# Attention layers: the high and low parts of q made by VectorE in place of GpSimd

## Chip, cores and metric

The kernel runs on one NeuronCore of a Trainium2 chip. The metric is the device time of one launch in microseconds (us); a run's time is that of its slowest core, here the only one. The engines are TensorE (PE in the rows; PEld is its loading of stationary operands), VectorE (DVE), ScalarE (ACT), GpSimd (POOL) and SyncE (SP), which issues most transfers. Each engine executes its own instructions in program order, and semaphores order the engines among each other.

## What is computed

The reference is one inference step of a decoder trunk of four layers (attention, a gated recurrence, a short gated convolution, attention), each followed by a SwiGLU feed-forward block, on 512 prompt tokens and 8 x 8 decode tokens, with model width 1024. All is float32. The change lies in the attention layers (0 and 3), cut here to what matters:

```python
qkv = h @ w_qkv + b_qkv
q = rope(q, pos); k = rope(k, pos)          # 16 query heads, 2 key/value heads, width 64
s = einsum(q, k) * 64 ** -0.5               # sliding window of 128 keys
p = softmax(concat([where(mask, s, -1e30), sink]))[..., :-1]
out = einsum(p, v) @ w_o + b_o
```

## The kernel before

The tokens are handled in two groups g of 288 columns (256 prompt tokens and 32 decode tokens). Activations lie transposed, features on the 128 partitions, so that a weight tile of 128 output features meets 288 columns. To get float32 accuracy out of single-pass matmuls every operand is split into a high part (the value rounded to fp32r, by a cast) and a low part (what the rounding left, by a subtraction); one product then takes three matmuls (lines 443 to 445: high by high, low by high, high by low). ScalarE casts each weight tile (`wh`, line 361), and the remainder `wl` is subtracted by VectorE (line 368) or, for the nine tiles from v and q of each attention layer and some others, by GpSimd in two halves of 128x512 (line 365).

In an attention layer a projection unit per head pair c and group g fills one PSUM bank (24 matmuls). Its evacuation `q_evac` (line 819) scales the bank (line 507), applies the rotary embedding in `rope` (VectorE at 752, 762 and 763, ScalarE at 757), which leaves the pair's rotated q in a scratch tile t, 128 partitions by 256 prompt columns, and then makes four pieces of 64 partitions by 256 columns. The first head's high part and its remainder go to the two halves of `mh`, the second head's remainder and high part to the two halves of `ml`. ScalarE casts one high part (line 832). GpSimd does the rest: a cast (827) and a subtraction (829) for the first head, in a side task of its own, and a subtraction (834) for the second.

A task per (g, c) then runs the attention itself: eight score matmuls on those pieces (lines 877 and 879), the masked minimum on VectorE (845), the exponential on ScalarE (851), after a GpSimd copy of the sink column into the tile P (883), reciprocal and normalisation on VectorE (855, 859), transposes of P on TensorE (894), a ScalarE copy to PT (896) and the product with v (910). Decode tokens take similar steps (930 to 966). Two P tiles and two PT tiles limit the tasks in flight. The output projection (`out_units`, evacuated at 656) follows and overlaps the last tasks.

The order of all instructions is set before the run by a list scheduler in the file (class `Sched`): each step of each task is yielded with an engine letter (P, A, D, G, S) and a guessed cost in us, and the scheduler picks for each engine the ready step of best priority. A step's guessed cost and engine therefore decide the order on every engine. Pools of eight PSUM banks, ten scratch tiles and six weight slots hold tasks back.

Of the kernel before, what the change touches and what calls it, by code (L numbers as in the profile page):

```python
# [8 lines left out]
F32 = mybir.dt.float32  # L9
# [5 lines left out]
D = 1024  # L15
# [5 lines left out]
HD = 64  # L21
# [3 lines left out]
NP = 256  # L25
# [220 lines left out]
def cA(n, sb=0, ap=0):  # L246
    return n / 1200 + 0.05 + 0.04 * sb + 0.09 * ap


def cD(n, ap=0):  # L250
    return n / 960 + 0.07 + 0.06 * ap


class Builder(Sched):
# [433 lines left out]
    def attention(self, layer, l):  # L688
        nc = self.nc
# [52 lines left out]
        def rope(ps, g, c, tmp, outs, key):  # L742
            b = bq(c)
            raw, rot = yield ("acq", self.scr, 2)
            yield from self.scaled(g, idx, raw, ps)
            yield ("free", self.pp, [ps])
            yield ("wait", [("const", l, "cos")])
            cs, sn = st["cs"][:, g, :], st["sn"][:, g, :]

            def part(out, src, b, t):  # L750
                yield ("D", cD(N, 1))
                nc.vector.scalar_tensor_tensor(out=out, in0=src, scalar=b, in1=t, op0=ALU.add, op1=ALU.mult)
            yield ("spawn", part(tmp, raw, b, cs), None, [("cos",) + key])
            yield ("A", 4 * cA(N, 1))
            for s in range(4):
                d = s ^ 1
                nc.scalar.copy(rot[32 * d:32 * d + 32, :], raw[32 * s:32 * s + 32, :])  # L757
            yield from part(rot, rot, self.cst(f"br{l}", c), sn)
            yield ("wait", [("cos",) + key])
            yield ("D", 0.44)  # L760
            v2 = lambda t: t.rearrange("p (a n) -> p a n", a=2)
            nc.vector.tensor_add(outs[0], tmp[:, :NP], rot[:, :NP])
            nc.vector.tensor_add(outs[1], v2(tmp[:, NP:]), v2(rot[:, NP:]))
            yield ("free", self.scr, [raw, rot])
            yield ("set", key)
# [52 lines left out]
        def q_evac(g, c, ps):  # L818


            [t] = yield ("acq", self.scr, 1)
            yield from rope(ps, g, c, t, (t[:, :NP], st["qs"][g][:, :, c, :]), ("qr", l, g, c))
            mh, ml = (m[:, c, :NP] for m in self.mid[g])

            def first():
                yield ("G", 0.97)
                nc.gpsimd.tensor_copy(mh[:HD], t[:HD, :NP])
                yield ("G", 0.7)
                nc.gpsimd.tensor_sub(mh[HD:], t[:HD, :NP], mh[:HD].bitcast(F32))
            yield ("spawn", first(), None, [("q1", l, g, c)])  # L830
            yield ("A", cA(NP, 1))
            nc.scalar.copy(ml[HD:], t[HD:, :NP])
            yield ("G", 0.7)
            nc.gpsimd.tensor_sub(ml[:HD], t[HD:, :NP], ml[HD:].bitcast(F32))
            yield ("wait", [("q1", l, g, c)])
            yield ("free", self.scr, [t])
            yield ("set", ("q", l, g, c))

# [140 lines left out]
        for c in range(KC):  # L979
            i = self.take()  # L980
            for g in range(2):
                def fn(prio, i=i, g=g, c=c):
                    pt = prio + AOFF[g]
                    self.spawn(task(g, c, pt), pt, 0.0, [("mp", l, g, c)])
                    if c == KC - 1:
                        for p in range(2):
                            ps = prio + SOFF[g] + p
                            self.spawn(stask(g, p, ps), ps, 0.0, [("ms", l, g, p)])
                    return self.unit(i, g, self.h, self.hkeys(g, idx), lambda ps: q_evac(g, c, ps), step=STEP)
                self.add(g, fn)  # L990
# [690 lines left out]
```

## Time and profile before

| | |
|---|---|
| time, median of 3 runs | 2393.68 us (2393.63 to 2394.46) |
| time of the profiled execution | 2392.32 us |
| span of the profiled execution | 2390.5 us |
| mean granted TensorE clock | 0.996 of full speed |
| busy, share of the span | PE 98%, DVE 70%, ACT 51%, POOL 28% |

The span runs from the first to the last instruction; the time also holds what lies around it, 1.8 us here. Layer 0's attention lies at the start of the span, up to about 200 us, layer 3's at about 1780 to 1975 us. A row of a wait names the engine and line that ended an engine's idle time. Busy time of PE counts pipelined matmuls that overlap, so a busy PE is not PE at its peak.

### The profile page before, as it was taken

The page shows a single profiled execution, that of the slowest core. Times are in us where ns is not written, and L with a number is a line of the kernel's source. Part 1 is how long each engine was busy: PE and PEld are TensorE (multiplying, and loading weights), DVE is VectorE, ACT ScalarE, POOL GpSimd, SP SyncE. Part 2 cuts the span into 40 slices and gives each one's busy share as a digit, 9 for nine tenths or more (in the row PEclk, how much of TensorE's full clock was granted, in tenths as well). Part 3 has the DMA queues.
Part 4 walks back from the last instruction along what each step waited for, and adds up shares of the span by engine and source line. Part 5 has one row for each costly group of instructions (what it writes and reads, how often), then busy time and mean ns, then how long its engine had stood idle before and what let it go on. Part 6 is the DMA issues. An engine that isn't in the chain of part 4 may idle for free.

```text
span 2390.5 us, 44197 instructions
## 1 busy us (share of the span) xinstructions
PE 2337.0 (98%) x17596; PEld 2300.3 (96%) x17596; DVE 1682.2 (70%) x3253; ACT 1226.8 (51%) x2546; POOL 659.1 (28%) x728
## 2 busy tenths in 40 slices
PE   8999999999999999999999999999999999999998
PEld 7889999999989999999999999999999899999998
DVE  8877848486896784848665578484867868757574
ACT  7864535355587552535422255353548845535353
POOL 5410414150451042424000004241415301333230
PEclk9999999999999999999999999999999999999999
DMA  5112232223222122322322212322242111413231
GB/s 186 46 51 65 71 106 87 86 100 103 63 80 92 53 97 83 103 81 90 109 89 80 82 62 79 99 93 94 87 132 86 46 54 36 137 58 115 71 107 49
DMA packets 64063, 203.69 MB, mean 85 GB/s; under 512 B 11040, under 2 KB 13904, under 8 KB 63840
## 3 DMA queue, kind: packets, MB, share of 16 engines
q1 hardware_dynamic: 62800, 199.52, 25.8%
q8 instruction: 138, 2.26, 0.4%
q0 software_dynamic: 336, 0.61, 0.1%
q10 hardware_dynamic: 720, 0.73, 0.1%
q14 instruction: 69, 0.57, 0.1%
HBM read 197.87 MB, written 4.94 MB: 85 GB/s over the span
## 4 chain that ended last, share of the span: by engine, by line
PE 80%; DVE 12%; ACT 6%; issue 1%; POOL 0%; DMA 0%; DVEq 0%; ACTq 0%; POOLq 0%
PE bank L443 14%; PE bank L444 14%; PE bank L445 14%; PE bank L1373 12%; PE bank L1375 11%; PE bank L1374 11%; DVE wl L418 1%; DVE s L1328 1%; ACT s L757 1%; PE bank L894 1%; DVE cv L1047 1%; ACT P L851 1%; PE bank L910 1%; ACT wh L361 1%; DVE hl L474 1%
## 5 line engine op out<-in xcount | busy, mean ns | idle before, releaser
L443 PE MATMUL bank<-mh,wh 128*128 128x288 f32 x1984 | 589.6, 297 | 4.6 <-ACT rg L1128 2.5
L444 PE MATMUL bank<-ml,wh 128*128 128x288 f32 x1984 | 585.6, 295 | 1.4 <-DVE ml L474 1.4
L445 PE MATMUL bank<-mh,wl 128*128 128x288 f32 x1984 | 583.6, 294 | 0.0
L443 PE MATMUL bank<-hh,wh 128*128 128x288 f32 x1344 | 407.1, 303 | 0.7 <-ACT hh L472 0.4
L444 PE MATMUL bank<-hl,wh 128*128 128x288 f32 x1344 | 399.2, 297 | 7.2 <-DVE hl L474 7.2
L445 PE MATMUL bank<-hh,wl 128*128 128x288 f32 x1344 | 398.4, 296 | 3.4 <-POOL wl L365 2.3
L443 PEld LDWEIGHTS bank<-mh,wh 128*128 128x128 f32 x1984 | 371.8, 187 | 7.0 <-ACT rg L1128 3.0
L361 ACT CAST wh<-raw 128x1024 fp32r<-128x1024 f32 (+2 forms) x217 | 219.2, 1012 | 310.0 <-PE bank L444 250.2
L444 PEld LDWEIGHTS bank<-ml,wh 128*128 128x128 f32 x1984 | 372.4, 188 | 2.3 <-DVE ml L474 1.9
L445 PEld LDWEIGHTS bank<-mh,wl 128*128 128x128 f32 x1984 | 373.5, 188 | 0.0
L418 DVE TENSOR_TENSOR wl<-raw,wh 128x512 fp32r<-128x512 f32 x380 | 347.8, 941 | 13.0 <-ACT wh L416 12.1
L659 DVE TENSOR_TENSOR x<-bank,x 128x288 f32<-128x288 f32 x224 | 102.0, 456 | 272.6 <-PE bank L445 272.6
L416 ACT CAST wh<-raw 128x512 fp32r<-128x512 f32 x380 | 228.5, 616 | 109.8 <-PE bank L444 107.4
L1375 PE MATMUL bank<-hh,wl 128*128 128x288 f32 x912 | 268.7, 295 | 4.8 <-DVE wl L418 4.8
L1373 PE MATMUL bank<-hh,wh 128*128 128x288 f32 x912 | 269.9, 296 | 0.0
L1374 PE MATMUL bank<-hl,wh 128*128 128x288 f32 x912 | 269.0, 295 | 0.0
L368 DVE TENSOR_TENSOR wl<-raw,wh 128x1024 fp32r<-128x1024 f32 (+2 forms) x187 | 222.9, 1192 | 58.8 <-ACT wh L361 56.9
L444 PEld LDWEIGHTS bank<-hl,wh 128*128 128x128 f32 x1344 | 254.7, 189 | 8.5 <-DVE hl L474 7.8
L445 PEld LDWEIGHTS bank<-hh,wl 128*128 128x128 f32 x1344 | 255.3, 190 | 4.8 <-POOL wl L365 3.2
L443 PEld LDWEIGHTS bank<-hh,wh 128*128 128x128 f32 x1344 | 254.4, 189 | 4.6 <-issue 2.2
L1381 ACT COPY s<-bank 128x288 f32<-128x288 f32 x228 | 91.2, 400 | 186.9 <-PE bank L1375 185.8
L1375 PEld LDWEIGHTS bank<-hh,wl 128*128 128x128 f32 x912 | 171.8, 188 | 6.0 <-DVE wl L418 6.0
(371 smaller groups left out, 5035.5 us busy)
## 6 DMA issues: line engine op xcount, KB each, us to landing
raw<-in_w SPq DMA_DIRECT2D x303, 512.0 KB
raw<-in_w SPq DMA_DIRECT2D x64, 448.0 KB
out_y<-x SPq DMA_DIRECT2D x12, 144.0 KB
x<-in_x SPq DMA_DIRECT2D x4, 288.0 KB
x<-in_x SPq DMA_DIRECT2D x2, 576.0 KB
ck<-in_ckt SPq DMA_DIRECT2D x4, 256.0 KB
cv<-in_cv SPq DMA_DIRECT2D x4, 256.0 KB
ca<-in_ca SPq DMA_DIRECT2D x2, 480.0 KB
```

The lines of the kernel that those rows point to most:

```text
L361: self.nc.scalar.copy(fh[:, z], r[:, z])
L368: self.nc.vector.tensor_sub(fl[:, z], r[:, z], fh[:, z].bitcast(F32))
L416: self.nc.scalar.copy(fh, src)
L418: self.nc.vector.tensor_sub(fl, src, fh.bitcast(F32))
L443: mm(out, lhsT=wh(k), rhs=xh(k), start=(k == 0), stop=False)
L444: mm(out, lhsT=wh(k), rhs=xl(k), start=False, stop=False)
L445: mm(out, lhsT=wl(k), rhs=xh(k), start=False, stop=(k == n - 1))
L659: nc.vector.tensor_add(x[:, m, :], ps[:, :N], x[:, m, :])
L1373: mm(ps[:, :N], lhsT=wh[:, k, :], rhs=xh[:, k, :], start=first and k == 0, stop=False, skip_group_check=not first)
L1374: mm(ps[:, :N], lhsT=wh[:, k, :], rhs=xl[:, k, :], start=False, stop=False, skip_group_check=not first)
L1375: mm(ps[:, :N], lhsT=wl[:, k, :], rhs=xh[:, k, :], start=False, stop=k == hk - 1, skip_group_check=not first)
L1381: nc.scalar.copy(c[n], ps[:, :N])
```

## The change

The three GpSimd instructions of a head pair become VectorE instructions with the same operands, and the side task `first` is dissolved: its two steps now stand in line ahead of ScalarE's cast. The scheduler is told 0.22 for the cast and `cD(NP)`, which is 0.337, for a subtraction, where it was told 0.97 and 0.7 of GpSimd. It is done 32 times in a run: 8 head pairs, 2 groups, 2 layers.

```diff
             mh, ml = (m[:, c, :NP] for m in self.mid[g])
 
-            def first():
-                yield ("G", 0.97)
-                nc.gpsimd.tensor_copy(mh[:HD], t[:HD, :NP])
-                yield ("G", 0.7)
-                nc.gpsimd.tensor_sub(mh[HD:], t[:HD, :NP], mh[:HD].bitcast(F32))
-            yield ("spawn", first(), None, [("q1", l, g, c)])
+            yield ("D", 0.22)
+            nc.vector.tensor_copy(mh[:HD], t[:HD, :NP])
+            yield ("D", cD(NP))
+            nc.vector.tensor_sub(mh[HD:], t[:HD, :NP], mh[:HD].bitcast(F32))
             yield ("A", cA(NP, 1))
             nc.scalar.copy(ml[HD:], t[HD:, :NP])
-            yield ("G", 0.7)
-            nc.gpsimd.tensor_sub(ml[:HD], t[HD:, :NP], ml[HD:].bitcast(F32))
-            yield ("wait", [("q1", l, g, c)])
+            yield ("D", cD(NP))
+            nc.vector.tensor_sub(ml[:HD], t[HD:, :NP], ml[HD:].bitcast(F32))
             yield ("free", self.scr, [t])
             yield ("set", ("q", l, g, c))
```

The scheduler's order moves on every engine within the two attention stretches, and outside them PE's order is the same. Lines after 834 carry numbers smaller by 3 in the changed kernel. Three places follow.

VectorE in layer 0, from the end of the first rope evacuation (s_87 is the rotated q of the first head pair, mh_102 and ml_103 are the pieces of group 0). Before:

```order
L762 TENSOR_TENSOR s_87<-s_87,s_89 128x256
L763 TENSOR_TENSOR qs_0_133<-s_87,s_89 128x2x16
L507 TENSOR_TENSOR s_92<-bank_65,rt_108 128x288
L752 SCALAR_TENSOR_TENSOR s_90<-s_92,cpack,cos_118 128x288
L507 TENSOR_TENSOR s_85<-bank_62,rt_107 128x288
```

and in the changed kernel:

```order
L762 TENSOR_TENSOR s_87<-s_87,s_89 128x256
L763 TENSOR_TENSOR qs_0_133<-s_87,s_89 128x2x16
L826 CAST mh_102<-s_87 64x256
L828 TENSOR_TENSOR mh_102<-s_87,mh_102 64x256
L507 TENSOR_TENSOR s_92<-bank_65,rt_108 128x288
L752 SCALAR_TENSOR_TENSOR s_90<-s_92,cpack,cos_118 128x288
L832 TENSOR_TENSOR ml_103<-s_87,ml_103 64x256
L507 TENSOR_TENSOR s_85<-bank_62,rt_107 128x288
```

Three VectorE instructions now stand among the evacuations of the next banks.

GpSimd at the same place (wl are weight remainders, P_0_135 and P_0_137 the two P tiles). Before:

```order
L365 TENSOR_TENSOR wl_80<-raw_72,wh_79 128x512 x2
L827 CAST mh_102<-s_87 64x256
L829 TENSOR_TENSOR mh_102<-s_87,mh_102 64x256
L834 TENSOR_TENSOR ml_103<-s_87,ml_103 64x256
L365 TENSOR_TENSOR wl_82<-raw_69,wh_81 128x512 x2
L883 COPY P_0_135<-cpack 128x4
```

and in the changed kernel:

```order
L365 TENSOR_TENSOR wl_80<-raw_72,wh_79 128x512 x2
L365 TENSOR_TENSOR wl_82<-raw_69,wh_81 128x512 x2
L880 COPY P_0_135<-cpack 128x4
L365 TENSOR_TENSOR wl_84<-raw_70,wh_83 128x512 x2
L880 COPY P_0_137<-cpack 128x4
```

What is left on GpSimd there is weight remainders and sink columns.

TensorE late in layer 0's attention, where the last prompt tasks meet the output projection (its rows have mh and wh; bank_62 and the like are PSUM banks). Before:

```order
L443 MATMUL bank_61<-mh_102,wh_73 128x288
L444 MATMUL bank_61<-ml_103,wh_73 128x288
L445 MATMUL bank_61<-mh_102,wl_74 128x288
L910 MATMUL bank_62<-PT_0_140,vtok_130 64x128 x8
L894 MATMUL bank_64<-ca_117,P_0_135 128x128 x4
L894 MATMUL bank_66<-ca_117,P_0_135 128x128 x4
L877 MATMUL bank_67<-kh_0_122,mh_104 128x256
```

and in the changed kernel:

```order
L445 MATMUL bank_68<-mh_102,wl_74 128x288
L891 MATMUL bank_67<-ca_117,P_0_137 128x128 x4
L891 MATMUL bank_64<-ca_117,P_0_137 128x128 x4
L891 MATMUL bank_65<-ca_117,P_0_135 128x128 x4
L891 MATMUL bank_62<-ca_117,P_0_135 128x128 x4
L907 MATMUL bank_63<-PT_0_140,vtok_130 64x128 x8
L907 MATMUL bank_61<-PT_0_139,vtok_130 64x128 x8
L443 MATMUL bank_66<-mh_102,wh_75 128x288
```

The transposes of two tasks now stand in one block, with both products with v right behind them; before, projection or score matmuls stood between a task's last transpose and its product.

## Rows read from the trace of the kernel before

**Rows 1.** The page's head: span, and busy time by engine.

```profile
span 2390.5 us, 44197 instructions
...
PE 2337.0 (98%) x17596; PEld 2300.3 (96%) x17596; DVE 1682.2 (70%) x3253; ACT 1226.8 (51%) x2546; POOL 659.1 (28%) x728
```

**Rows 2.** Busy us by stretch: PE, PEld, DVE, ACT, POOL, clock, DMA share, GB/s.

```profile
30.00:160.00 130.00, 121.69 (x1016) 111.54 (x1015) 115.86 (x374) 110.90 (x306) 56.35 (x81) 0.99 0.22 67
1810.00:1940.00 130.00, 125.40 (x1059) 115.11 (x1058) 109.33 (x373) 106.86 (x300) 47.87 (x75) 1.00 0.18 59
...
80.00:90.00 10.00, 9.05 (x70) 7.98 (x67) 9.65 (x35) 8.88 (x28) 6.82 (x10) 1.00 0.08 19
...
1890.00:1900.00 10.00, 9.47 (x91) 7.81 (x88) 9.77 (x31) 8.87 (x25) 3.37 (x6) 1.00 0.40 134
```

**Rows 3.** PE's waits from 30 to 160 us: us in total, times, longest.

```profile
PE bank L894 <- DVE P L859: 4.1, 6, 1.4
...
PE bank L877 <- POOL mh L829: 1.0, 1, 1.0
PE bank L944 <- DVE P L859: 0.9, 2, 0.5
```

**Rows 4.** PE's waits from 1810 to 1940 us.

```profile
PE bank L894 <- DVE P L859: 1.4, 3, 0.5
...
PE bank L944 <- DVE P L859: 0.4, 1, 0.4
```

**Rows 5.** GpSimd's groups over the span: busy us, mean ns; idle before.

```profile
L834 POOL TENSOR_TENSOR ml<-s,ml 64x256 fp32r<-64x256 f32 x32 | 26.0, 811 | 6.4 <-ACT ml L832 4.3
L829 POOL TENSOR_TENSOR mh<-s,mh 64x256 fp32r<-64x256 f32 x32 | 25.8, 807 | 2.5
...
L827 POOL CAST mh<-s 64x256 fp32r<-64x256 f32 x32 | 16.1, 503 | 111.5 <-DVE s L762 111.4
```

**Rows 6.** VectorE in order of time: start, duration, undisturbed instructions.

```profile
40.25 0.41 DVE L774 TENSOR_TENSOR kl<-s,kh 64x256 fp32r<-64x256 f32 x1
40.59 0.44 DVE L507 TENSOR_TENSOR s<-bank,rt 128x288 f32<-128x288 f32 x1
...
141.28 0.35 DVE L859 TENSOR_SCALAR P<-P,st 128x256 f32<-128x256 f32 x1
141.55 0.42 DVE L474 TENSOR_TENSOR ml<-bank,mh 128x256 fp32r<-128x256 f32 x1
```

**Rows 7.** VectorE and GpSimd in order of time, where both run.

```profile
34.32 1.09 DVE L752 SCALAR_TENSOR_TENSOR s<-s,cpack,cos 128x288 f32<-128x288 f32 x1
...
35.81 0.52 DVE L752 SCALAR_TENSOR_TENSOR s<-s,cpack,cos 128x288 f32<-128x288 f32 x1
...
34.36 0.74 POOL L829 TENSOR_TENSOR mh<-s,mh 64x256 fp32r<-64x256 f32 x1
```

**Rows 8.** PE in order of time: its waits, in brackets their length and end.

```profile
59.87 0.86 PE L894 MATMUL bank<-ca,P 128*128 128x128 f32 x5 [0.57 <-DVE P L859]
...
71.09 0.30 PE L894 MATMUL bank<-ca,P 128*128 128x128 f32 x1 [1.50 <-ACT P L851]
72.39 0.41 PE L894 MATMUL bank<-ca,P 128*128 128x128 f32 x2 [0.99 <-DVE P L859]
...
1884.07 0.41 PE L894 MATMUL bank<-ca,P 128*128 128x128 f32 x2 [0.43 <-DVE P L859]
...
1942.57 1.09 PE L910 MATMUL bank<-PT,vtok 128*64 128x128 f32 x14 [0.57 <-ACT PT L896]
```

**Rows 9.** GpSimd and VectorE ahead of the wait at 71 us.

```profile
69.60 2.49 POOL L365 TENSOR_TENSOR wl<-raw,wh 128x512 fp32r<-128x512 f32 x2 [0.39 <-POOL mh L829]
...
69.71 2.53 DVE L859 TENSOR_SCALAR P<-P,st 128x128 f32<-128x128 f32 x2
...
46.37 0.55 DVE L859 TENSOR_SCALAR P<-P,st 128x128 f32<-128x128 f32 x2
```

**Rows 10.** The stretch behind that wait, one us: clock 0.50 of full speed.

```profile
73.00:74.00 1.00, 1.00 (x6) 1.00 (x5) 0.93 (x6) 0.81 (x3) 0.00 (x0) 0.50 0.91 176
```

## The prediction

> **What bounds the kernel now.** I read the page's head first: PE is busy 2337.0 us of a span of 2390.5 us, so all of PE's idle time together is 53.5 us [rows 1]. The change touches two stretches only, so the next view is busy time by stretch. From 30 to 160 us (layer 0) PE is idle 130 - 121.69 = 8.3 us, from 1810 to 1940 us (layer 3) 130 - 125.40 = 4.6 us [rows 2]. These 12.9 us are nearly all that a change here can win, 0.5% of the time, since the matmuls themselves stay the same. VectorE is the next engine: busy 115.86 and 109.33 us of 130, against 56.35 and 47.87 of GpSimd [rows 2]. The waits of PE tell what VectorE's delay costs: 4.1 + 0.9 us in layer 0 and 1.4 + 0.4 us in layer 3, 6.8 us together, end when VectorE has normalised P; a single one, of 1.0 us, ends with GpSimd's low part of q [rows 3, 4].
>
> **What leaves GpSimd.** 32 casts and 64 subtractions, 16.1 + 25.8 + 26.0 = 67.9 us of its busy time [rows 5]. None of it is time by itself, since GpSimd waits more than it works here. Three things come with it.
>
> The wait on GpSimd's low part goes: 1.0 us [rows 3]. In its place the first scores wait for VectorE's three instructions; these stand two to four places behind the rope sum in the order shown, while on GpSimd the three take 0.50 + 0.81 + 0.81 = 2.1 us by their means [rows 5], one after the other. I take the whole 1.0 us as won.
>
> VectorE's own instructions get faster. An L752 that takes 0.52 us alone took 1.09 us while GpSimd's L829 ran [rows 7]. Going through VectorE's rows of both layers I find 21 such, from that one at 34.32 us to one at 1890.41 us, that ran long beside one of the three instructions and beside no weight remainder; what they took over their undisturbed length sums to 7.4 us, 5.5 of it in layer 0.
>
> Some of these were normalisations that PE waited for. Five of PE's waits, the first at 59.87 us (0.57 us) and the last at 1884.07 us (0.43 us) [rows 8], follow a normalisation stretched by 0.25 to 0.5 us in this way; taking each wait or its stretch, whichever is shorter, gives 1.9 us. With the 1.0 us above, **2.9 us are won**.
>
> **What VectorE gets.** A subtraction of 64x256 took 0.41 us there, and the next instruction started 0.34 us after it [rows 6]. The cast of 64x256 on VectorE does not occur. Its nearest row is the normalisation of 128x256, one input and all in SBUF, with 0.27 us to the next start [rows 6]; the other end is the subtraction's 0.34. I take 0.27, because a single input is what the two share. Per head pair this is 0.27 + 2 x 0.34 = 0.95 us, 32 x 0.95 = 30.4 us in all, 15.2 a layer; less the 7.4 us it is 23.0 us more of VectorE's time on top of 115.86 + 109.33 = 225.2 us. That leaves 260 - 248.2 = 11.8 us idle of the 34.8 us now, most of it in layer 3.
>
> None of this work stands on PE's path as such. It delays what is queued behind it on VectorE: evacuations of banks and normalisations. Two bounds for what PE then waits. If the waits on normalisations grow as VectorE's busy time does, 6.8 x 23.0 / 225.2 = 0.7 us. If they grow as its idle time shrinks, as in a queue, 6.8 x (34.8 / 11.8 - 1) = 13.3 us. The rows nearest to the state to come are the slices in which VectorE is at 95% or more already. There are seven of 10 us, the first and the last shown; PE is idle in them 0.95, 0, 1.41, 0, 0, 0.53 and 0.53 us, 0.49 us a slice, and over all 26 slices 12.9 / 26 = 0.50 us [rows 2]. A loaded VectorE has not meant a waiting PE, because the planner puts projection matmuls under the softmax. So I take **0.7 us lost** and keep 13.3 us for the range.
>
> **What the new order costs.** In the changed order the transposes of two tasks stand together and the products with v come right behind them, at two places in layer 0 and one or two in layer 3. The row like it is the end of layer 3, where the products waited 0.57 us for ScalarE's copy [rows 8]. At that price three places cost 1.7 us; nothing at the other end, since the first task's product covers part of the copy. I take the middle, **0.9 us lost**. ScalarE's work is the same; its cast of q now comes behind two VectorE steps, 0.6 us later, and no row shows PE waiting for that cast. The weight loads on SP's queue keep their order but for three that move by a few places, and GpSimd's weight remainders and sink columns come earlier; no wait of PE in rows 3 or 4 ends with either, so I cost both at nothing. What hides the loads is that raw weights lie ready ahead of ScalarE's casts.
>
> **Sum.** 2392.32 us, the profiled execution's own time (span 2390.5 us), - 2.9 + 0.7 + 0.9 = 2391.0 us. The median of the runs lies 1.36 us above that execution, so 2392.4 us on the scale of the runs: no change, by 0.2% (4.8 us), which is about what a measurement of this kernel can tell.
>
> **Rivals.** *VectorE becomes the bound (slower).* The place is layer 0, where VectorE has 14.1 us of idle time and gets 15.2 - 5.5 = 9.7 us net. The point is where a backlog reaches past one task: both P tiles are then held by tasks that wait for VectorE, and PE runs out of projections to put under them. The price goes up to the queue's 13.3 us: -2.9 + 13.3 + 0.9 = +11.3, 2405.0 us; half of the queue's price gives 2398.3 us. For it: VectorE would be at 97% in layer 0. Against it: the seven loaded slices. Chance 0.18.
>
> *The long waits of layer 0 dissolve (faster).* At 71 and 72 us PE waited 1.50 + 0.99 us [rows 8] behind a pair of normalisations that took 2.53 us where such a pair takes 0.55 us, because GpSimd's weight remainder ran beside them [rows 9]; that remainder came late, right behind GpSimd's q work. After this wait the granted clock fell to 0.50, the 1.2 GHz level, for three slices of one us, of which the first is shown [rows 10]; at half the clock they cost another 1.5 us of matmul time. Without q on GpSimd the remainder starts some 2 us earlier, under other instructions. Then 2.5 + 1.5 us go as well: -2.9 - 4.0 + 0.7 + 0.9 = -5.3, and with no loss from order or queue -6.9, so 2386.8 to 2388.4 us. Against it: another normalisation can meet another remainder. Chance 0.20.
>
> *The new instructions are held by the weight remainders (slower).* Each layer has nine tiles whose remainder GpSimd makes in two halves, 36 in all. At 69.71 us two halves held two normalisations by 2.53 - 0.55 = 2.0 us, 1.0 us a half [rows 9]. By my count of stretched rows half of the 36 hold a VectorE instruction today. If the other half hold one of the new ones, VectorE gets 18 us more, of which the 11.8 us of idle time takes up most; 6.2 us reach PE: -1.3 + 6.2 = +4.9, 2398.6 us. Against it: the remainders run where VectorE already has something of this kind in front of them, so a new instruction mostly takes the place of another. Chance 0.08.
>
> The Trainium skill (SBUF — State Buffer, section Who interferes with whom) has a rule that stands behind this rival: a VectorE instruction with two SBUF inputs, or in a mode that takes both ports, and a GpSimd instruction that reads SBUF exclude each other for the whole instruction, whichever starts second. The trace agrees as far as it goes, with 1.09 us against 0.52 us [rows 7]. By that rule all 96 new instructions are of the kind that can be held, and it speaks against the change as long as weight remainders stay on GpSimd; it also says that the 48 a layer that leave GpSimd hold nobody any more.
>
> That the change would not do what it says is excluded by the order: GpSimd loses 96 instructions and VectorE gets 96.
>
> **How the numbers follow.** No change 0.54, the two slower rivals 0.18 + 0.08 = 0.26, the faster one 0.20. The forecast is that of the likeliest, 2392.4 us. The range runs from 2386 us, just below the faster rival's end, to 2402 us, between the half and the whole price of the queue: it leaves out about 0.08 on each side. The likeliest case by itself spans 2391 to 2397 us: 2.9 us won whole or by half, 0 to 1.7 us for the order, nothing to a quarter of the queue's price.
>
> **What would show it.** Right: VectorE's busy time in the two stretches some 23 us up and GpSimd's some 68 us down; cast and subtraction near 0.35 and 0.41 us when undisturbed; no wait of PE for q of more than some tenths; PE idle 10 to 15 us over both stretches; everything outside them as it was. Wrong: waits on P of over 12 us, or evacuations of banks that PE waits for (then VectorE bounds); new subtractions of 1 us and more beside L365; a clock at 0.50 at a new place; or stretches with less than 7 us of idle PE.

## The result, and the profile after

The changed kernel takes 2406.47 us (median of 4 runs, 2405.4 to 2410.19) where the kernel before, run beside it, takes 2393.8 us: a ratio of 1.006, 95% interval 1.0044 to 1.0077. That is 0.6% slower, clear of the noise, and above the range's end of 2402 us. The forecast was no change. The time lies near the 2405.0 us of the rival in which VectorE becomes the bound; that its terms came out otherwise is told below.

The page's head of the changed kernel, whose profiled execution took 2405.4 us, answers to [rows 1]:

```profile
span 2403.6 us, 44163 instructions
...
PE 2343.3 (97%) x17596; PEld 2304.8 (96%) x17596; DVE 1709.7 (71%) x3349; ACT 1228.0 (51%) x2546; POOL 596.7 (25%) x632
```

VectorE's share over the span moves by one point and PE's falls by one, so the head shows nothing of the cause. Busy time by stretch, with the columns of [rows 2], does:

```profile
30.00:160.00 130.00, 118.92 (x979) 108.12 (x977) 120.59 (x396) 106.06 (x289) 22.12 (x32) 0.99 0.21 67
1810.00:1940.00 130.00, 120.09 (x973) 109.57 (x972) 119.77 (x395) 103.34 (x284) 17.60 (x29) 0.97 0.18 55
...
40.00:50.00 10.00, 6.73 (x41) 5.89 (x40) 9.67 (x32) 7.10 (x19) 3.25 (x4) 0.83 0.50 155
...
70.00:80.00 10.00, 7.71 (x64) 6.91 (x64) 9.80 (x32) 6.79 (x21) 4.29 (x5) 1.00 0.31 96
...
1850.00:1860.00 10.00, 7.05 (x53) 6.35 (x52) 9.84 (x35) 6.13 (x19) 2.90 (x4) 1.00 0.17 52
```

PE is now idle 11.1 us in layer 0 and 9.9 us in layer 3, where it was 8.3 and 4.6 us. In [rows 2] two slices with VectorE over 95% had PE busy 9.05 and 9.47 us of ten; the three slices here have it at 6.73, 7.71 and 7.05. Of the 26 slices of ten us in the two stretches 14 now have VectorE at 95% or more, and PE is idle 1.16 us a slice in them, against 0.39 in the other twelve.

The two fixed stretches cut the stages off before they end. From 20 us to the residual sum that ends layer 0's attention, and from the one ahead of layer 3's to the one behind it, both kernels have the same matmuls (1356 or 1357 and 1441 records). Before:

```profile
20.00:198.00 178.00, 166.88 (x1357) 154.43 (x1356) 141.90 (x428) 130.24 (x346) 59.49 (x83) 0.99 0.22 69
1790.72:1973.39 182.67, 176.24 (x1441) 163.93 (x1440) 138.06 (x431) 132.89 (x353) 55.89 (x82) 1.00 0.21 63
```

and in the changed kernel:

```profile
20.00:203.81 183.81, 169.01 (x1356) 154.90 (x1356) 153.05 (x475) 130.73 (x346) 25.01 (x35) 0.99 0.21 66
1793.61:1984.82 191.21, 179.47 (x1441) 166.38 (x1440) 154.36 (x479) 134.03 (x353) 23.39 (x34) 0.98 0.20 61
```

The two stages grow by 5.81 + 8.54 = 14.35 us; the rest of the span gives 1.25 us back, together the 13.1 us by which the span grew. PE's idle time in them grows from 17.55 to 26.54 us, by 9.0. The other 5.4 us are matmuls that take longer, 2.8 of them by the clock: read in slices of one us, PE's busy time lost 1.4 + 3.1 us to a granted clock below full speed, where it lost 1.7 us before. Layer 3, which had no such place before, now has two of some three us at a granted clock of 0.50, the 1.2 GHz level, both behind waits of PE.

What ended PE's waits, from 30 to 160 us (us in total, times, longest), against [rows 3]:

```profile
PE bank L891 <- DVE P L856: 3.6, 7, 1.0
PE bank L874 <- DVE ml L832: 3.2, 2, 1.8
...
PE bank L874 <- DVE mh L828: 0.9, 1, 0.9
PE bank L941 <- DVE P L856: 0.7, 1, 0.7
```

and from 1810 to 1940 us, against [rows 4]:

```profile
PE bank L891 <- DVE P L856: 6.1, 6, 2.4
...
PE bank L874 <- DVE ml L832: 0.9, 1, 0.9
```

Waits on the normalised P are 3.6 + 0.7 + 6.1 = 10.4 us where they were 6.8 (11.7 over the whole stages). Waits on q's low parts are 3.2 + 0.9 + 0.9 = 5.0 us where GpSimd cost 1.0: all of them now end with VectorE, though e2 below shows that waits of this length come with the new order and not with the engine.

VectorE's new instructions, in order of time; first an undisturbed pair, then a subtraction that met a weight remainder:

```profile
51.90 0.29 DVE L826 CAST mh<-s 64x256 fp32r<-64x256 f32 x1
52.22 0.42 DVE L828 TENSOR_TENSOR mh<-s,mh 64x256 fp32r<-64x256 f32 x1
52.67 0.46 DVE L507 TENSOR_TENSOR s<-bank,rt 128x288 f32<-128x288 f32 x1
...
53.60 0.42 DVE L474 TENSOR_TENSOR ml<-bank,mh 128x256 fp32r<-128x256 f32 x1
54.05 0.42 DVE L832 TENSOR_TENSOR ml<-s,ml 64x256 fp32r<-64x256 f32 x1
54.50 0.23 DVE L852 RECIPROCAL st<-st 128x2 f32<-128x2 f32 x2
...
61.60 0.42 DVE L474 TENSOR_TENSOR ml<-bank,mh 128x256 fp32r<-128x256 f32 x1
61.95 0.15 DVE L852 RECIPROCAL st<-st 128x2 f32<-128x2 f32 x1
...
66.79 1.52 DVE L832 TENSOR_TENSOR ml<-s,ml 64x256 fp32r<-64x256 f32 x1
```

Read the distance from one start to the next. Behind L826 it is 0.32 us and behind each subtraction 0.45, where [rows 6] have 0.34 behind an L774 of the same size. L474 holds VectorE for 0.35 us at 61.60, but for 0.45 us at 53.60, where L832 follows. So a head pair takes 0.32 + 2 x 0.45 + 0.10 = 1.32 us of VectorE, not 0.95. The subtraction at 66.79 is one of six among the 64 that were held (the others take 0.90 to 1.41 us). PE waited for it; its row stands here between the two longest waits of the two stretches:

```profile
44.66 0.33 PE L874 MATMUL bank<-kh,ml 128*128 128x128 f32 x1 [1.79 <-DVE ml L832]
...
68.36 0.39 PE L874 MATMUL bank<-kh,ml 128*128 128x256 f32 x1 [1.38 <-DVE ml L832]
...
1831.72 0.93 PE L891 MATMUL bank<-ca,P 128*128 128x128 f32 x3 [2.44 <-DVE P L856]
```

The two longest waits stand behind held rows of VectorE as well, a new subtraction and three instructions that were there before:

```profile
41.01 1.38 DVE L828 TENSOR_TENSOR mh<-s,mh 64x256 fp32r<-64x256 f32 x1
42.41 1.37 DVE L774 TENSOR_TENSOR kl<-s,kh 64x256 fp32r<-64x256 f32 x1
...
1824.83 1.60 DVE L752 SCALAR_TENSOR_TENSOR s<-s,cpack,cos 128x288 f32<-128x288 f32 x1
1826.36 1.51 DVE L774 TENSOR_TENSOR kl<-s,kh 64x256 fp32r<-64x256 f32 x1
```

GpSimd makes weight remainders during both pairs, two halves from 40.79 us and two from 1824.83 us. None of these waits comes at the end of a stage: the projections of layer 0 run on to 128 us, those of layer 3 to 1906 us.

### The profile page after: what moved, and what is told of

Same layout as the page of the kernel before. It is cut to its first block, busy times and chain, and to the rows that moved or that the text cites. A ratio compares the mean times of both kernels' runs of the same rounds, so it can differ in the third digit from the quotient of the medians.

```text
span 2403.6 us, 44163 instructions
## 1 busy us (share of the span) xinstructions
PE 2343.3 (97%) x17596; PEld 2304.8 (96%) x17596; DVE 1709.7 (71%) x3349; ACT 1228.0 (51%) x2546; POOL 596.7 (25%) x632
## 4 chain that ended last, share of the span: by engine, by line
PE 78%; DVE 15%; ACT 5%; issue 1%; POOL 0%; DMA 0%; DVEq 0%; ACTq 0%; POOLq 0%
PE bank L443 14%; PE bank L444 14%; PE bank L445 14%; PE bank L1370 11%; PE bank L1372 11%; PE bank L1371 11%; DVE P L842 1%; DVE s L1325 1%; DVE wl L418 1%; ACT s L757 1%; DVE P L856 1%; DVE cv L1044 1%; DVE s L752 1%; DVE ml L474 1%; PE bank L891 1%
```

## The experiments

Three causes stood against each other: VectorE's added work (PE waits for what is queued behind it), the new order of instructions, and the new subtractions held by GpSimd's weight remainders. All times below are medians of runs beside the kernel before on the same chip; where two experiments are compared, the ratios are, at 1% = 23.9 us.

### Engine and order taken apart

e1_order_kept leaves the scheduler's table as before, so PE's order is the old one, and moves the engine alone:

```diff
                 yield ("G", 0.97)
-                nc.gpsimd.tensor_copy(mh[:HD], t[:HD, :NP])
+                nc.vector.tensor_copy(mh[:HD], t[:HD, :NP])
...
-                nc.gpsimd.tensor_sub(mh[HD:], t[:HD, :NP], mh[:HD].bitcast(F32))
+                nc.vector.tensor_sub(mh[HD:], t[:HD, :NP], mh[:HD].bitcast(F32))
...
-            nc.gpsimd.tensor_sub(ml[:HD], t[HD:, :NP], ml[HD:].bitcast(F32))
+            nc.vector.tensor_sub(ml[:HD], t[HD:, :NP], ml[HD:].bitcast(F32))
```

> The planner is told what it was told before (GpSimd steps of 0.97 and 0.7), and only the instructions are issued on VectorE: PE's order is that of the kernel before, VectorE has the load of the change. If the load on VectorE is the cause: 2402 to 2409 us, with PE's waits on P and on q's low part as long as in the change, over 15 us in both stretches. If the new order is the cause: 2391 to 2395 us. If it is the place of the three instructions right behind the rope sum: about halfway, near 2398 us.

e2_engine_kept is the reverse: the change's steps and costs, with `nc.gpsimd` kept in all three:

```diff
-            def first():
-                yield ("G", 0.97)
-                nc.gpsimd.tensor_copy(mh[:HD], t[:HD, :NP])
...
+            yield ("D", 0.22)
+            nc.gpsimd.tensor_copy(mh[:HD], t[:HD, :NP])
+            yield ("D", cD(NP))
+            nc.gpsimd.tensor_sub(mh[HD:], t[:HD, :NP], mh[:HD].bitcast(F32))
```

> The planner is told what the change tells it (VectorE steps of 0.22 and 0.337), and the instructions are issued on GpSimd: the order of the change, the load of before. Load on VectorE as the cause: 2392 to 2397 us. Order as the cause: 2402 to 2409 us.

e1 took 2411.24 us against 2391.37, a ratio of 1.0081 (1.0068 to 1.0093), a little more than expected; e2 2392.49 us, 1.0007 (0.9998 to 1.0016). The loss goes with the engine. The new order by itself costs little, and with VectorE loaded it is no worse than the old one (1.0060 against 1.0081).

What ended PE's waits in e2, from 20 to 210 us and, behind the dots, from 1790 to 1990 us, holds the change's order fixed:

```profile
PE bank L874 <- POOL ml L832: 2.0, 3, 1.1
PE bank L891 <- DVE P L856: 1.8, 3, 1.0
PE bank L874 <- POOL mh L828: 1.3, 1, 1.3
...
PE bank L874 <- POOL ml L832: 2.9, 4, 1.3
PE bank L891 <- DVE P L856: 2.9, 3, 1.3
...
PE bank L941 <- DVE P L856: 1.3, 2, 1.0
```

In the new order PE waits 6.2 us for q's low parts with GpSimd, more than the 5.0 us with VectorE, and the kernel is hardly slower for it. What the engine adds at the same order is on P, 11.7 us in the change's stages against 6.0 here, and in the clock: the slices of one us show no place below full speed in e2's stages, and 4.5 us lost in the change's.

e11_told_more tests whether the scheduler only had too low a cost: the change with 0.42, 0.55 and 0.55 in the three yields.

```diff
-            yield ("D", 0.22)
+            yield ("D", 0.42)
             nc.vector.tensor_copy(mh[:HD], t[:HD, :NP])
-            yield ("D", cD(NP))
+            yield ("D", 0.55)
```

> The change, with the planner told 0.42, 0.55 and 0.55 for the three steps (what they occupy VectorE for, with what they hold and are held) in place of 0.22, 0.337 and 0.337. If the planner's too low cost is what made the change slow, since it plans VectorE as if it had time: 4 to 10 us faster than the change. If the work itself is too much: within 3 us of the change.

2404.26 us against 2391.93, 1.0055 (1.0043 to 1.0067): as slow as the change within the intervals, so too low a guess of the cost isn't what made it slow.

### How much work, and which

e3_cast_only moves the cast alone, e5_second_sub the last subtraction alone, e9_first_pair the cast and the first subtraction, e10_cast_second the cast and the last subtraction. Each takes its lines from the change; for e5:

```diff
-            yield ("G", 0.7)
-            nc.gpsimd.tensor_sub(ml[:HD], t[HD:, :NP], ml[HD:].bitcast(F32))
+            yield ("D", cD(NP))
+            nc.vector.tensor_sub(ml[:HD], t[HD:, :NP], ml[HD:].bitcast(F32))
```

> Only the cast moves to VectorE, planned as such, the two subtractions stay on GpSimd. If each instruction costs by the time it takes on VectorE: the cast takes 0.28 of the change's 0.28 + 0.42 + 0.42 us, a quarter, so +3 us, 2396 to 2398 us. If what costs is being held by GpSimd's weight remainders: less, since the held rows of the change are subtractions, 2393 to 2395 us. If the order costs: anywhere from 2390 to 2405 us.

> Only the second head's subtraction moves to VectorE, planned as such; cast and first subtraction stay on GpSimd. If the change's 14 us grow evenly with the work moved (cast at nothing by the run with the cast alone): half of them, +6 to +8 us. If VectorE has slack that takes the first part and the rest is dear: +0 to +3 us.

> Cast and first subtraction on VectorE, planned as such and in line as in the change; the second subtraction stays on GpSimd. If VectorE has slack for about half of the work and the rest is dear: +1 to +5 us, like the next run. If the pair that stands right behind the rope sum is what is dear, whatever the rest: +9 to +14 us.

> Cast and second subtraction on VectorE, the first subtraction on GpSimd: as much work on VectorE as in the run with the first pair, at other places. Slack for about half of the work: within 3 us of that run. The pair behind the rope sum as the cause: -2 to +2 us against the kernel before.

| | us | before | ratio, 95% interval |
|---|---|---|---|
| e3, cast | 2392.94 | 2391.37 | 1.0005 (0.9997 to 1.0014) |
| e5, last subtraction | 2389.51 | 2391.89 | 0.9991 (0.9982 to 1.0) |
| e9, cast and first subtraction | 2400.39 | 2391.93 | 1.0041 (1.0025 to 1.0057) |
| e10, cast and last subtraction | 2401.09 | 2391.93 | 1.0036 (1.0024 to 1.0048) |
| the change, all three | 2406.47 | 2393.8 | 1.006 (1.0044 to 1.0077) |

The cast alone and the last subtraction alone cost nothing that can be told from noise, the cast and a subtraction some 9 us, all three 14 us; which of the two subtractions goes with the cast does not matter, so the place right behind the rope sum is not what is dear. The first subtraction alone and the two subtractions without the cast were not run. Some 9 us is more than the 1 to 5 us expected from slack for half of the work. The sums fit a queue that fills, not a fixed price per instruction; each run also has an order of its own.

### The load without any reader

e4_load_doubled leaves q to GpSimd, and VectorE executes the three instructions a second time into tiles that nobody reads, so no wait of PE can end with them:

```diff
                 nc.gpsimd.tensor_copy(mh[:HD], t[:HD, :NP])
+                nc.vector.tensor_copy(st["dm"][:HD], t[:HD, :NP])
...
+                nc.vector.tensor_sub(st["dm"][HD:], t[:HD, :NP], st["dm"][:HD].bitcast(F32))
...
+            nc.vector.tensor_sub(st["dn"][:HD], t[HD:, :NP], t[HD:, :NP])
```

> The kernel before, with GpSimd still making q's parts, and VectorE issuing a cast and two subtractions of the same size per head pair into tiles that nobody reads, at the places where GpSimd's are issued; the planner is told nothing. No one waits for their results. If time comes from what is queued behind them on VectorE: as slow as the change or slower, 2404 to 2412 us, since GpSimd's instructions still hold VectorE too. If it comes from the scores waiting for q's parts on VectorE's queue: 2394 to 2398 us.

e6_load_straight does the same work with every operand on partitions 0 to 63:

```diff
-                nc.vector.tensor_sub(st["dm"][HD:], t[:HD, :NP], st["dm"][:HD].bitcast(F32))
+                nc.vector.tensor_sub(st["dn"][:HD], t[:HD, :NP], st["dm"][:HD].bitcast(F32))
...
-            nc.vector.tensor_sub(st["dn"][:HD], t[HD:, :NP], t[HD:, :NP])
+            nc.vector.tensor_sub(st["dn"][:HD], t[:HD, :NP], t[:HD, :NP])
```

> The run with VectorE's load doubled, with its three extra instructions reading and writing partitions 0 to 63 alone, so that none begins at another partition than its neighbours; lengths and places are the same, one of the two subtractions reads other data. If an instruction that crosses partitions holds VectorE until the one in front of it is through: the extra instructions cost less VectorE time, next starts 0.34 us behind a subtraction instead of 0.45 us, and the time falls by 5 to 15 us against that run. If length alone counts: the same within 3 us.

e4 took 2423.58 us against 2391.37, 1.0127 (1.0114 to 1.0141), with the largest sum of waits on P, here from 20 to 210 us (P is normalised at L863 there):

```profile
PE bank L898 <- DVE P L863: 12.2, 11, 3.9
```

Nobody reads the new results and the kernel is 30 us slower: the price is paid by what stands behind them on VectorE. It is more than the change's, and more than the 2404 to 2412 us expected; GpSimd's q instructions are still there beside it, and the two added subtractions average 618 and 582 ns, against 511 and 489 in the change. e6 took 2415.29 us against 2391.89, 1.0101 (1.0086 to 1.0117), 6 us less than e4. The same place in both, VectorE in e4:

```profile
60.48 0.75 DVE L863 TENSOR_SCALAR P<-P,st 128x128 f32<-128x128 f32 x1
61.26 0.42 DVE L832 TENSOR_TENSOR dm<-s,dm 64x256 fp32r<-64x256 f32 x1
61.70 0.35 DVE L863 TENSOR_SCALAR P<-P,st 128x256 f32<-128x256 f32 x1
```

and in e6:

```profile
59.65 0.75 DVE L863 TENSOR_SCALAR P<-P,st 128x128 f32<-128x128 f32 x1
60.33 0.41 DVE L832 TENSOR_TENSOR dn<-s,dm 64x256 fp32r<-64x256 f32 x1
60.66 0.34 DVE L863 TENSOR_SCALAR P<-P,st 128x256 f32<-128x256 f32 x1
```

With the output on the other half of the partitions the subtraction starts 0.78 us after its predecessor, not 0.68, and the next one 0.44 us later, not 0.33. These 0.2 us a subtraction, 64 times, are 13 us of VectorE's time that no duration shows.

### GpSimd's weight remainders

e7_before_zero_wl and e8_after_zero_wl take GpSimd's remainders of nine tiles a layer out of the kernel before and of the change; GpSimd writes zeros, which reads nothing:

```diff
+        self.zerow |= set(range(iv, iv + 9))
...
+                        if i in self.zerow:
+                            self.nc.gpsimd.memset(fl[:, y].bitcast(F32), 0.0)
+                        else:
+                            self.nc.gpsimd.tensor_sub(fl[:, y], r[:, y], fh[:, y].bitcast(F32))
```

> The kernel before, with the remainders of the nine attention weight tiles a layer left out: GpSimd writes zeros in their place, at the same places of the order, and reads nothing. If GpSimd's remainders hold VectorE today: faster than before by 2 to 8 us, with no stretched VectorE rows beside them. If not: the same within 2 us.

> The change with the same remainders left out and zeros written. If the change is slow because its subtractions meet the remainders: the gap between this run and the kernel before with zeros falls to under 5 us. If it is slow because VectorE has too much work: the gap stays at 10 to 15 us, and the run is faster than the change only by what the kernel before gains in the same way.

e7: 2380.15 us against 2391.89, 0.9954 (0.9941 to 0.9966). e8: 2388.42 us, 0.9985 (0.9976 to 0.9993). The remainders cost the kernel before 11 us, though no wait of PE in rows 3 and 4 ends with one. Without them q on VectorE costs 7.4 us, about half of the change's 14.4, where under 5 or 10 to 15 us were expected. The traces show where it goes: in e8's two stages PE waits 2.3 + 0.7 + 1.2 + 1.3 = 5.5 us for P, not longer than e7's 6.5, and not at all for q's parts; PE is idle 3.2 us longer, in shorter waits, and 3.3 us go to the clock, which stands at 0.50 at two places in e8 and nowhere in e7's stages. Part of the 7.4 us can belong to the new order, which e2 puts at 1.7. So with nothing to hold the new subtractions their own work still costs something, but the longer waits on P of the change need the remainders as well. To see whether these waits need the holds or only a fuller VectorE, the remainders were kept and moved. e12_wl_on_vector is the kernel before with the nine remainders a layer on VectorE, by one line; e13_all_on_vector is the change with the same line gone:

```diff
-        self.poolw |= set(range(iv, iv + 9))
```

> The kernel before, q's parts on GpSimd, and the remainders of the nine attention weight tiles a layer on VectorE in place of GpSimd. VectorE gets 18 x 1.14 = 20.5 us and is no longer held by the remainders, which cost it about as much by the rows of before. If holding is the dearer of the two, because it falls on instructions that PE waits for: 3 to 8 us faster than before. If work is: 3 to 10 us slower.

> The change's kernel with the nine attention weight remainders of each layer moved to VectorE as well, so that in the attention stretches GpSimd computes nothing that reads two operands of on-chip memory and cannot hold VectorE there. Beside it stands the run of the kernel before with the same remainders moved (2379.9 us, 0.9951 of before); both carry the same remainders on VectorE, and they differ by q's cast and two subtractions alone. Theory 1, the change loses by VectorE's own added work (normalisations queue behind it): 7 to 15 us above that run, 0.998 to 1.0015 of before, and TensorE still waits on P behind L856's successor for over 5 us between 30 and 160 us. Theory 2, the change loses only by the new subtractions being held by GpSimd's remainders: with the holds gone it is within 3 us of that run, 0.994 to 0.9965 of before, and the waits on P stay under 2 us. In between, both have a part, and the distance from 2379.9 us tells the part of VectorE's own work.

e12 took 2379.9 us against 2391.93, 0.9951 (0.9939 to 0.9963): **it beats both kernels**, by 0.5% and 1.1%, by more than the 3 to 8 us expected at best. e13 took 2395.93 us against 2392.37, 1.0014 (1.0005 to 1.0023). Busy time by stretch in e12:

```profile
30.00:160.00 130.00, 125.50 (x1074) 114.51 (x1072) 114.03 (x392) 111.19 (x313) 38.48 (x68) 1.00 0.18 56
1810.00:1940.00 130.00, 125.85 (x1068) 114.92 (x1067) 106.00 (x369) 104.03 (x294) 36.65 (x60) 1.00 0.17 54
```

VectorE does the remainders and is busy less than in [rows 2], 114.03 and 106.00 us against 115.86 and 109.33: on GpSimd they cost VectorE more than on VectorE itself. Over the whole span it is 1676.8 us against 1682.2, with 18 instructions more. PE's waits on P from 20 to 210 us shrink to a single one of 0.3 us; one of 1.6 us ends with a reciprocal ahead of P.

e13 differs from e12 by q's three instructions, and by the order that goes with them, and is 15 us slower (1.0014 against 0.9951), so the first of its two theories stands and the second falls. Its waits on P from 20 to 210 us, in the profiled execution, the fastest of the run (2391.34 us):

```profile
PE bank L941 <- DVE P L856: 9.0, 2, 5.2
...
PE bank L891 <- DVE P L856: 0.8, 2, 0.5
```

and three slices ahead of them and at them:

```profile
90.00:100.00 10.00, 10.00 (x83) 9.60 (x82) 9.60 (x39) 8.54 (x27) 0.47 (x2) 1.00 0.01 2
...
110.00:120.00 10.00, 5.72 (x57) 4.38 (x55) 9.63 (x36) 7.72 (x23) 0.19 (x1) 0.98 0.18 53
120.00:130.00 10.00, 6.37 (x51) 4.97 (x49) 9.82 (x34) 8.97 (x26) 0.31 (x2) 0.84 0.19 54
```

VectorE is as full at 90 us as at 110, and PE is busy throughout at 90 us and a little over half at 110. Until then the order had other matmuls to put under the softmax: the last projection of layer 0 starts at 108.2 us and the first of the output projection at 138.3. In between, PE waited for VectorE's backlog twice, 3.8 and 5.2 us. Behind these waits the granted clock is 0.50 again; e13's two stages lose 5.7 us to the clock and e12's none.

What stays open: in the change itself six held subtractions add 5.1 us to VectorE, and the three longest waits of PE in the stretches end with rows that were held or stood behind held ones. How much of the 14 us is the new work as such, how much the holds that it meets, can't be told by subtraction, since e13, whose new subtractions are never held (means 419 and 421 ns), has the remainders as more work on VectorE.

## Why the prediction was wrong, point by point

- **The queue behind VectorE** is the step that failed: "So I take 0.7 us lost and keep 13.3 us for the range". What VectorE's load costs was measured at 19 us with the old order (e1), 15 us beside remainders on VectorE (e13 against e12) and 7.4 us with the remainders left out (e8 against e7), not 0.7. The argument for 0.7 was seven slices at 95% or more in which PE waited no more than elsewhere, 0.49 us a slice. With more work queued the same kind of slice reads 1.16 us in the change, in fourteen of them, and 0.45 in e8's eleven. So the busy share of a slice did not tell how much is queued there: e13's slices at 90 and at 110 us are equally full, and PE stands in the second alone. The load also cost PE some of its clock, for which the sum has no term in its likeliest case.
- **The queue's bound** of 13.3 us was no measure of it either. Its formula takes the waits on P from 6.8 to 20 us; they are 10.4. It counted on 11.8 us of idle VectorE, and 19.6 are left in the two stretches. That the time comes out near 2405 us is in part luck: 3.6 us more on P in the stretches, 4.0 on q and 5.4 of longer matmuls make up most of it, where 13.3 on P less 2.9 won were counted.
- **VectorE's cost per pair** was too low: 0.95 us taken, 1.32 measured, so 42.2 us for 32 pairs instead of 30.4, and 5.1 us of holds on top, 47.3 in all. The idle time of VectorE in the two stretches was 34.8 us. The nearest row was an L774 that reads and writes one half of the partitions, with the next instruction free to start 0.34 us later; the change's subtractions read one half and write the other. The kernel before had a nearer row, the other head's L774 on the other half of the partitions:

```profile
1823.74 0.45 DVE L774 TENSOR_TENSOR kl<-s,kh 64x256 fp32r<-64x256 f32 x1
1824.22 0.46 DVE L507 TENSOR_TENSOR s<-bank,rt 128x288 f32<-128x288 f32 x1
```

Behind it the next instruction starts 0.03 us after its end; in [rows 6] it starts 0.07 us before the end. The Trainium skill (VectorE: DVE Perf Modes, section Two Vector instructions with no wait between them) gives a rule, as a model: an instruction starts only when all earlier ones have finished if one of its inputs starts in another group of 32 partitions than the first input of the last instruction that read the same memory, or its output in another than the last output written there. The rows agree on both sides of a subtraction, 0.45 against 0.35 us ahead of it and 0.45 against 0.34 behind it. The cast was sized well: 0.28 us long and 0.32 to the next start, where 0.27 was taken.
- **The 2.9 us won** did not show. The 1.0 us wait on GpSimd's q became 5.0 us on VectorE's, by the new order, as e2's 6.2 us on GpSimd's tell. The stretched instructions did get shorter: VectorE's busy time grew by 27.5 us though the new instructions are busy 9.1 + 16.4 + 15.7 = 41.2 us, so 13.7 us were refunded, where 7.4 were counted; PE's waits on P did not get shorter by it.
- **The new order** at 0.9 us fits: e2 puts it at 1.7 us, with an interval from 0.5 us gained to 3.8 us lost.
- **The rival of the held instructions** had a real mechanism and too many cases: six subtractions were held where 18 halves were feared, and no cast was (289 ns the longest; in e1 one took 1.20 us beside a remainder). By the Trainium skill's rule on the shared port (SBUF — State Buffer, section Who interferes with whom) the 64 subtractions could be, and the casts in a mode that takes both ports; the trace has 1.41 us against 0.42 for a subtraction that was. What the rival missed is that the remainders already cost the kernel before 11 to 12 us, as e7 and e12 show.
- **The faster rival** did not occur: the waits at 71 and 72 us went, and others of 1.79 and 1.38 us came at 44 and 68 us, both behind rows that a remainder held, as the argument against it said.
- **The rival in which VectorE becomes the bound** has the direction and the total. Its mechanism, PE running out of projections, shows in e13 but not in the change, whose longest waits in the stretches come while projections are still to be done. It also missed that layer 3 would lose more than layer 0, 8.5 against 5.8 us, for all the 20.7 us of VectorE's idle time there.

## To carry to other kernels

Before work is moved to an engine that is 87% busy in a stage, compare the work with that engine's idle time in the stage in start-to-start distances, not durations, and don't take slices in which a full engine did no harm for a proof that more work will do none: here the same share of 95% went with 0.49 us of PE's waiting a slice before and 1.16 after. Ask of the engine that is to be relieved what its other instructions do to the busy one: here the three q instructions were better left on GpSimd and the weight remainders moved instead (e12, 0.9951), the opposite of the change. And before a wait is put down to an engine, look at what the new order does to it with the old engine: q's waits grew in e2 as well.

## What the runs showed of the hardware

- A 64x256 subtraction that reads one half of the partitions and writes the other takes 0.42 us as a row, and VectorE loses 0.1 us ahead of it and 0.1 us behind it; 6 us of e4's time went when the operands were put on one half.
- A GpSimd subtraction of 128x512 (1.39 us in the mean) can hold a VectorE instruction of two operands in SBUF for as long: 1.41 and 1.52 us instead of 0.42. A cast with its one operand in SBUF took 1.20 us beside such a subtraction in e1, where 0.28 is usual. Moved to VectorE, 18 tiles' worth of remainders made VectorE's busy time 5.4 us smaller, and the kernel 12 us faster.
- Some waits of PE are followed by about three us at a granted clock of 0.50. In the change the one of 2.44 us at 1831 us is: four slices of one us from there have 0.55, 0.50, 0.50 and 0.75, with PE busy 0.28, 1, 1 and 1 us of them, so 1.4 us of clock are lost on top of the wait. The waits of 1.07 and 1.16 us at 1855 and 1859 us are not followed by such a fall.
